# Values and gates of the short sequence: from ten column groups of 256 in the long mLSTM to six of 430 in the long attention

## The chip, the cores and the metric

The kernel runs on one core of a Trainium2 chip. The metric is the device time of one execution in microseconds (us); three runs of the kernel before are given. A separate profiled execution supplies the trace, with its own time.

The engines are named as the profile names them: PE is TensorE (matmuls), PEld its weight loads, DVE is VectorE, ACT is ScalarE, POOL is GpSimd, and SP is the engine whose queue issues most DMAs.

## The reference

One encoder layer is computed for two sequences, `x_prompt` (1024 tokens, called A or long here) and `x_sample` (512 tokens, B or short), all in float32 with a width of 1024:

```python
h = rms_norm(x, pre_w)
cols = h @ w_in                                  # 1024 columns in, 12,304 out
m_qk, m_v, m_o, m_z, m_i, m_f, a_qkv, a_z, gate = split(cols)
y_m = mlstm_mixer(m_qk, m_v, m_o, m_i, m_f, ...) * silu(m_z)      # conv of 3 over m_qk, two directions, chunks of 128
y_a = dilated_attention(a_qkv, rel_table) * silu(a_z)             # three dilations, 8 heads each, width 64
p_m, p_a = y_m @ w_pm, y_a @ w_pa
g = sigmoid(gate)
out = (g[0] * p_m + g[1] * p_a) @ w_out
return x + rms_norm(out, post_w)
```

The change touches three slices of `cols` for the short sequence: the gates `m_i, m_f` (16 columns), the mLSTM's values `m_v` (1024 columns) and the attention's values (1536 columns of `a_qkv`): 2576 columns in all.

## The kernel before

Every float32 product of the dense part is made of three matmuls on parts in the matmul's reduced float type: each operand is split in a high part (ACT copies, rounding) and a low part (DVE subtracts), and `mm3` (L193 to L198) issues high x high, high x low and low x high. In the profile these are the lines L196, L197 and L198.

The program runs in stages. First the dense products of A, with a two-level fast scheme for blocks of four (from the start to about 950 us). Then four stages in which a scan or an attention leads and the rest is filled in: the long mLSTM (`N.mlstm(A, ...)`, L1840), the long attention (`N.attend(A, ...)`, L1845), the short mLSTM (L1855) and the short attention (L1870), and an end of projections.

*The fill.* `Fill` (L114 to L174) is a list of units. A unit is one weight tile or several and a generator; each `yield` is a step. The leading stage calls `fill(share)` at fixed places of its round, and `fill.stage(steps, shares)` says how many steps a stage is to make in all. The numbers are `STEPS = (310, 232, 194, 290, 86)` (L1643), and `SHORT = 736` (L1642) counts all steps of the short sequence's own units. The long mLSTM has 64 rounds (4 heads, 8 chunks, two directions), each of which makes its fill in thirds; the long attention has 96 rounds of one tile each and three more to drain, with one share each (`att_round`, L1382). PE and SP run in the order in which the program is written; the other engines' order comes from the framework's planner.

*The weights of the fill.* `load_w` (L244) fetches a raw tile through `N.side` (SP's queue in the two mLSTM stages, POOL's in the long attention) into one of two `wraw` buffers. `split_w` (L251) splits it into one of the places `wsplit`: ACT writes the high part (L256), DVE the low part (L257). There are three places. `Fill.load` (L125) keeps the split tiles at most two ahead of those taken, and not more than there are places beyond `base`; the raw fetch is one more ahead.

*The short units* (`short_units`, L788 to L835), in order: 8 units of attention queries and keys (`att`), ten value units, 4 of `az`, 6 of `att`, 16 convolutions (`conv`), 8 pairs of `z` and `o` (together they make the gated factor G), 10 of `att`, and 16 output gates. All but the value units have eight steps with one weight tile of 128 columns, which is the stationary operand, and three matmuls of 512 columns a step. They write a PSUM bank of `ps_d`, of which there are two.

*The value units* (`value_unit`, L752 to L786): here the tokens are stationary and the weights move. Each of ten units has 256 columns (the first 272, with the gates) in two weight tiles of four rows of blocks each. For each of four token tiles it makes 8 x 3 matmuls, with a step after every second block: 16 steps of six matmuls a unit, 160 in all. After the last block `put` (L773) evacuates: for the mLSTM's values a high part (ACT, L779) and a low part (DVE, L780) go into one `sw` buffer and by DMA to `T.vs`; for the attention's a copy (ACT, L784) goes to `T.av`. `N.sw` rotates over four buffers; taking one issues a DMA still pending on it, and pending DMAs are issued by `tick` after `lag` rounds (two in the long mLSTM, three in the long attention).

*The convolution* (`conv_unit`, L676): POOL zeroes the two edge columns of `sraw` (L679, L680), ACT copies the PSUM bank into `sraw` (L797), then ACT L683, DVE L685 twice, ACT L686 and DVE L687. `sraw` is at the same time the only buffer of `N.sg`, which holds the factor of a `z` and `o` pair (L1835, L1836).

*Around it.* In the round of the long mLSTM, POOL, ACT and DVE prepare the next round (`front`, L1019) while PE makes the present one (`core`, L1054); the row values come by DMA (`rows`, L1009, tile `rw`), the state is updated on DVE (`cf`, L1085), ACT and DVE. In the long attention each tile goes through four stages, one round apart: products (`lg`), softmax (DVE L1287, ACT L1291), transposes (`pt`, L1298) and output (`o`, L1310). In both the last tile or head calls for the loads of the next stage.

## Time and profile before

| what | value |
|---|---|
| median of 3 runs | 2275.14 us (2273.26 to 2279.46) |
| profiled execution, its own time | 2274.2 us |
| its span, first to last instruction | 2272.4 us |
| PE busy | 2247.1 us, 99% of the span |
| DVE, ACT, POOL busy | 1502.9, 1130.3, 693.9 us |
| granted TensorE clock, mean | 0.998 |
| value units (first and last fetch of `w_v`) | 1005.1 to 1194.6 us |
| weights by DMA from `w_v` | 20 of 512 or 544 KB |

The profile's first part gives each engine's busy time, where matmuls are pipelined, so that a busy PE need not run at its best. The second cuts the span into forty slices. The fourth follows the work that ended last back to its start. The fifth groups instructions by line and shape. A window gives the busy time of each engine in a stretch of the span; the timeline gives single instructions with their start.

### The profile page before, as it was taken

What the parts mean: (1) busy time and instruction counts of PE and PEld (TensorE: products, weight loads), DVE (VectorE), ACT (ScalarE), POOL (GpSimd) and SP (SyncE); (2) the same over time, 40 slices, a digit from 0 to 9 for tenths busy, and PEclk for the clock granted to TensorE, in tenths of its full rate; (3) what the DMA queues carried; (4) which work ended last, traced back from release to release, by engine and by line L of the source; (5) the groups of instructions that cost most, each with busy time, mean ns of one, the idle gap of its engine ahead of it and who ended that gap; (6) DMA issues with size and microseconds to landing.
All of it is one profiled execution on the core that took longest, in us unless ns stands there. A gap on an engine that the chain in (4) does not pass through costs nothing.

```text
span 2272.4 us, 36227 instructions
## 1 busy us (share of the span) xinstructions
PE 2247.1 (99%) x12610; PEld 1970.5 (87%) x12610; DVE 1502.9 (66%) x2866; ACT 1130.3 (50%) x2376; POOL 693.9 (31%) x1002
## 2 busy tenths in 40 slices
PE   9999999999999999999999999999999999999998
PEld 8999888888888888889999889998888888888886
DVE  7765577678776556457776856665498844656673
ACT  6432244344444334366667666766665644545331
POOL 2000333333333223236566511011256522221220
PEclk9999999999999999999999999999999999999999
DMA  3652455543322223384674788987688698785661
GB/s 122 166 134 76 171 205 193 194 167 121 112 111 103 83 84 139 112 313 141 221 232 138 205 246 233 250 214 210 197 271 275 207 277 239 215 270 188 234 234 72
DMA packets 227952, 418.83 MB, mean 184 GB/s; under 512 B 24793, under 2 KB 131481, under 8 KB 227770
## 3 DMA queue, kind: packets, MB, share of 16 engines
q1 hardware_dynamic: 201144, 323.70, 45.3%
q0 software_dynamic: 23024, 80.23, 10.9%
q10 hardware_dynamic: 3602, 12.59, 1.4%
q8 instruction: 100, 1.64, 0.3%
q14 instruction: 82, 0.67, 0.1%
HBM read 296.44 MB, written 128.39 MB: 187 GB/s over the span
## 4 chain that ended last, share of the span: by engine, by line
PE 88%; issue 3%; DMA 3%; DVE 2%; ACT 2%; POOL 1%; SPq 0%; POOLq 0%; DVEq 0%; ACTq 0%
PE d L198 13%; PE d L197 13%; PE d L196 13%; PE dense L196 11%; PE dense L197 11%; PE dense L198 11%; PE o L1310 4%; PE pt L1298 2%; PE lg L1275 2%; DMA rw<-rw_a 1%; PE num L196 1%; PE num L198 1%; PE num L197 1%; PE a L996 1%; PE kv L196 1%
## 5 line engine op out<-in xcount | busy, mean ns | idle before, releaser
L196 PE MATMUL dense<-H,wh 128*128 128x512 f32 x672 | 277.0, 412 | 0.2 <-DVE r L1092 0.2
L198 PE MATMUL dense<-H,wl 128*128 128x512 f32 x672 | 263.7, 392 | 0.0
L197 PE MATMUL dense<-H,wh 128*128 128x512 f32 x672 | 263.1, 392 | 0.0
L197 PE MATMUL d<-Hl,phla 128*128 128x512 f32 x608 | 236.5, 389 | 0.0
L198 PE MATMUL d<-Hh,phla 128*128 128x512 f32 x608 | 236.5, 389 | 0.0
L196 PE MATMUL d<-Hh,phla 128*128 128x512 f32 x608 | 236.5, 389 | 0.0
L257 DVE TENSOR_TENSOR wl<-wraw,wh 128x1024 fp32r<-128x1024 f32 (+1 forms) x127 | 157.9, 1243 | 101.1 <-ACT wh L256 100.3
L256 ACT ACTIVATE wh<-wraw 128x1024 fp32r<-128x1024 f32 (+1 forms) x130 | 137.0, 1054 | 81.6 <-PE dense L197 31.2
L198 PE MATMUL d<-Hh,phlb 128*128 128x512 f32 x456 | 177.4, 389 | 0.0
L196 PE MATMUL d<-Hh,phlb 128*128 128x512 f32 x456 | 177.4, 389 | 0.0
L197 PE MATMUL d<-Hl,phlb 128*128 128x512 f32 x456 | 177.4, 389 | 0.0
L1287 DVE CUSTOM_DVE_ANT_0 ls<-lg,bias 128x256 f32<-128x256 f32 (+1 forms) x288 | 93.6, 362 | 122.7 <-PE lg L1275 58.1
L1291 ACT ACTIVATE ls<-ls,nm 128x256 f32<-128x256 f32 (+1 forms) x288 | 129.9, 453 | 84.0 <-DVE nm L1289 67.0
L635 POOL TENSOR_TENSOR psum_w<-pw_raw 128x512 f32<-128x512 f32 x38 | 56.1, 1477 | 363.8 <-DMA pw_raw<-w_in 202.2
L198 PEld LDWEIGHTS dense<-H,wl 128*128 128x128 f32 x672 | 126.2, 188 | 28.4
L197 PEld LDWEIGHTS dense<-H,wh 128*128 128x128 f32 x672 | 127.0, 189 | 16.4
L196 PEld LDWEIGHTS dense<-H,wh 128*128 128x128 f32 x672 | 126.6, 188 | 16.8 <-PE dense L198 0.6
L196 PE MATMUL d<-vhi,Hh 128*128 128x322 f32 x448 | 140.9, 314 | 0.3
L198 PE MATMUL d<-vhi,Hl 128*128 128x322 f32 x448 | 140.2, 313 | 0.5 <-DVE Hl L361 0.3
L197 PE MATMUL d<-vlo,Hh 128*128 128x322 f32 x448 | 139.7, 312 | 0.8 <-DVE vlo L434 0.8
L198 PEld LDWEIGHTS d<-Hh,phla 128*128 128x128 f32 x608 | 114.1, 188 | 23.7
L197 PEld LDWEIGHTS d<-Hl,phla 128*128 128x128 f32 x608 | 114.1, 188 | 23.7
(563 smaller groups left out, 6237.9 us busy)
## 6 DMA issues: line engine op xcount, KB each, us to landing
pw_raw<-w_in SPq DMA_DIRECT2D x76, 512.0 KB
aqk_a<-pwk SPq DMA_DIRECT2D x48, 512.0 KB
wraw<-w_in SPq DMA_DIRECT2D x45, 512.0 KB
wraw<-w_in POOLq DMA_DIRECT2D x31, 512.0 KB, 5.6
aqk_b<-sw SPq DMA_DIRECT2D x48, 256.0 KB
wraw<-w_pm POOLq DMA_DIRECT2D x24, 512.0 KB, 6.2
wraw<-w_out POOLq DMA_DIRECT2D x24, 512.0 KB, 4.0
wraw<-w_v SPq DMA_DIRECT2D x18, 512.0 KB
```

The costliest lines, as they stand in the source:

```text
L196: nc.tensor.matmul(out, lh, rh, start=start, stop=False)
L197: nc.tensor.matmul(out, lh, rl, start=False, stop=False)
L198: nc.tensor.matmul(out, ll, rh, start=False, stop=stop)
L256: self.splits = (nc.scalar.activation(hi[:, :n], raw[:, :n], AF.Copy), (self.lows or nc.vector).tensor_sub(lo[:, :n], raw[:, :n], hi[:, :n ...
L257: (self.lows or nc.vector).tensor_sub(lo[:, :n], raw[:, :n], hi[:, :n].bitcast(F32)))
L635: self.nc.gpsimd.tensor_add(s[:, 0], ws[1][:, 0], ws[1][:, 1])
L996: nc.tensor.matmul(p[:, c - c0], kT[:, ct, c * P:(c + 1) * P], qT[:, ct, c * P:(c + 1) * P], start=ct == 0, stop=ct == 1)
L1275: nc.tensor.matmul(lg[:, hh, c:c + w], q[hh][:, qs], z[:, k0:k0 + w], start=z is k[hh], stop=z is not k[hh])
L1287: nc.vector.tensor_tensor_reduce(out=ls[:, hh], in0=ts["lg"][hh], in1=bt[:, hh], scale=1.0, scalar=NEG, op0=OP.add, op1=OP.max, accum_out= ...
L1291: nc.scalar.activation(ls[:, hh], ls[:, hh], AF.Exp, bias=nm[:, hh:hh + 1], accum_out=ot[:, 128 + hh:129 + hh])
L1298: nc.tensor.transpose(pp[:, hh * nk + x], ts["ls"][:, hh, x * P:(x + 1) * P], self.ident)
L1310: nc.tensor.matmul(po[:, hh * 64:hh * 64 + 64], pt[:, hh * nk + x], v[:, kt[x], c0 + hh * 64:c0 + hh * 64 + 64], start=x == 0, stop=x == n ...
```

## The change

The ten value units become one unit, `value_units`, with six groups of 430 columns (the gates first, then the mLSTM's and the attention's values; 2580 columns of which the last four are padding and not computed). Each group has four weight tiles of two rows of blocks and 860 columns. The four token tiles of a group, and the groups after each other, overlap: a tile's second half is made in the same slots as the next tile's first half, so that two tiles are open in the two banks, and each weight tile is released after the fourth token tile has used it. A step is one block, three matmuls; there are 192.

For this unit two more places of split weights are laid over `X0` and `X1`, which the long mLSTM uses and the long attention does not, and they are dropped when the unit has ended (`extra`, `retired`).

The order of the short units changes: after the first 8 `att` units come eight convolutions (heads 0 and 1), each followed by one of the 6 `att` and first 2 `az` units; then two `az`, seven pairs of `z` and `o`, the values, the other eight convolutions, and the last pair. The rest is as it was. With `STEPS` the values begin 4 steps after the start of the long attention.

`sraw` is zeroed once, so the convolution no longer zeroes its edges, and `N.sg` gets a buffer of its own. The keys of the DMAs to `vs` and `av` no longer name the unit. The weight ring is 1024 columns wide, not 1088.

```diff
-VG = 256 + 16
-RING = 4 * VG
+VS, NV = 430, 2580
+RING = 1024
...
 # Fill.load
+            if any(self.net.wsplit[0][0] is x for x in self.net.retired):
+                self.net.wsplit.pop(0)
+                continue
...
-    def conv_unit(self, u, T, raw, w):
+    def conv_unit(self, u, T, raw, w, edges=True):
...
-        nc.gpsimd.memset(raw[:, 0:1], 0.0)
-        nc.gpsimd.memset(raw[:, S + 1:S + 2], 0.0)
+        for c in (0, S + 1) if edges else ():
+            nc.gpsimd.memset(raw[:, c:c + 1], 0.0)
...
+    def value_units(self, T):
+        nc = self.nc
+        groups = NV // VS
+
+        def put(t, lo, hi, ps):
+            ts = slice(t * P, (t + 1) * P)
+            if lo == 0:
+                nc.scalar.activation(self.gates_of(T, t), ps[:, 0:16].rearrange("p (j h) -> p j h", h=4), AF.Copy)
+            a0, a1 = max(lo, 16), min(hi, 16 + D)
+            if a0 < a1:
+                parts, x = [self.sw(F32R) for _ in range(2)], ps[:, a0 - lo:a1 - lo]
+                h, l = (z[:, :a1 - a0] for z in parts)
+                nc.scalar.activation(h, x, AF.Copy)
+                nc.vector.tensor_sub(l, x, h.bitcast(F32))
+                for i, z in enumerate((h, l)):
+                    self.put(("vs", T.S), T.vs[i, ts, a0 - 16:a1 - 16], z.bitcast(F32), parts[i])
+            a0 = max(lo, 16 + D)
+            if a0 < hi:
+                z = self.sw()
+                nc.scalar.activation(z[:, :hi - a0], ps[:, a0 - lo:hi - lo], AF.Copy)
+                self.put(("av", T.S), T.av[ts, a0 - 16 - D:hi - 16 - D], z[:, :hi - a0], z)
+
+        def make(weights):
+            fill = weights.__self__
+            w, p = {}, {}
+            for slot in range(8 * groups + 2):
+                for i in (slot // 2 - 1, slot // 2):
+                    g, t = divmod(i, 4)
+                    if not 0 <= i < 4 * groups:
+                        continue
+                    kp = slot - 2 * i
+                    if t == 0:
+                        w[g, kp] = [x.rearrange("p (k c) -> p k c", c=VS) for x in weights(g == kp == 0)]
+                    if kp == 0:
+                        p[i] = self.ps_d.tile([P, BLK], F32, name="dense")
+                    wk, ts = w[g, kp], slice(t * P, (t + 1) * P)
+                    lo, hi = VS * g, min(VS * (g + 1), 16 + D + 1536)
+                    for k in (2 * kp, 2 * kp + 1):
+                        h = self.hT[k // 4]
+                        self.mm3(p[i][:, :hi - lo], (h[0][:, k % 4, ts], h[1][:, k % 4, ts]),
+                                 (wk[0][:, k % 2, :hi - lo], wk[1][:, k % 2, :hi - lo]), k == 0, k == KT - 1)
+                        if k == KT - 1:
+                            put(t, lo, hi, p.pop(i))
+                        if t == 3 and k % 2:
+                            fill.release()
                         yield
...
+            self.retired = self.extra
+        return Unit([(self.a["w_v"][i], 2, VS) for i in range(4 * groups)], make)
...
 # short_units, conv
-                self.sg()
                 nc.scalar.activation(self.sraw[:, 1:1 + BLK], p, AF.Copy)
-                self.conv_unit(u, T, self.sraw, w)
+                self.conv_unit(u, T, self.sraw, w, False)
...
-        units = [x for u in range(4) for x in pair(u)] + [self.value_unit(u, T) for u in (0, 4, 1, 5, 2, 6, 3, 7, 8, 9)]
-        units += [az(i) for i in range(4)] + [x for u in range(4, 7) for x in pair(u)]
-        for h in range(4):
-            units += [conv(u + 2 * h + ct) for u in (U_MQ, U_MK) for ct in range(2)]
+        units = [x for u in range(4) for x in pair(u)]
+        others = [x for u in range(4, 7) for x in pair(u)] + [az(i) for i in range(4)]
+        zo = [x for i in range(8) for x in (z_unit(i), o_unit(i))]
+        convs = [conv(u + 2 * h + ct) for h in range(4) for u in (U_MQ, U_MK) for ct in range(2)]
         for i in range(8):
-            units += [z_unit(i), o_unit(i)]
+            units += convs[i:i + 1] + others[i:i + 1]
+        units += others[8:] + zo[:14] + [self.value_units(T)] + convs[8:] + zo[14:]
...
-SHORT = 736
-STEPS = (310, 232, 194, 290, 86)
+SHORT = 768
+STEPS = (316, 260, 192, 290, 86)
...
-                sraw = sp.tile([P, BLK + 2], F32R, name="sraw")
-                N.sg, N.sraw = Rot(N, [sraw[:, :BLK]]), sraw.bitcast(F32)
+                N.sraw = sp.tile([P, BLK + 2], F32, name="sraw")
+                nc.gpsimd.memset(N.sraw, 0.0)
+                N.sg = Rot(N, [sp.tile([P, BLK], F32R, name="sg")])
...
                 N.side = nc.gpsimd
+                extra = [N.take(x) for x in ("X0", "X1")]
+                extra = [[x[:, 1024 * i:1024 * (i + 1)] for i in range(2)] for x in extra]
+                N.extra = [x[0] for x in extra]
+                N.wsplit += extra
...
                 N.side = nc.sync
+                assert len(N.wsplit) == 3
```

More of the change, by code (lines that the diff above doesn't have):

```diff
@@ L750, in unit @@
         return Unit([(self.a["w_in"][u],)], make)
-    def value_unit(self, u, T):
+    def value_units(self, T):
         nc = self.nc
-        W = VG if u == 0 else 256
-        srcs = [((self.a["w_v0"][kh] if u == 0 else self.a["w_v"][2 * u + kh]), 4, W) for kh in range(2)]
-        def make(weights):
-            w = [[x.rearrange("p (k c) -> p k c", c=W) for x in weights(kh == 0)] for kh in range(2)]
-            for t in range(T.n):
-                ps = self.ps_d.tile([P, BLK], F32, name="dense")
-                ts = slice(t * P, (t + 1) * P)
-                for k in range(KT):
-                    wh, wl = w[k // 4]
-                    hi, lo = self.hT[k // 4]
-                    self.mm3(ps[:, :W], (hi[:, k % 4, ts], lo[:, k % 4, ts]), (wh[:, k % 4], wl[:, k % 4]), k == 0,
-                             k == KT - 1)
-                    if k == KT - 1:
-                        put(t, ts, ps)
-                    if k % 2:
-                        yield
-        def put(t, ts, ps):
-            if u == 0:
-                nc.scalar.activation(self.gates_of(T, t), ps[:, 256:VG].rearrange("p (j h) -> p j h", h=4), AF.Copy)
-            if u < 4:
-                of = self.sw(F32R)
-                z = of.rearrange("p (a c) -> p a c", a=2)
-                nc.scalar.activation(z[:, 0], ps[:, :256], AF.Copy)
-                nc.vector.tensor_sub(z[:, 1], ps[:, :256], z[:, 0].bitcast(F32))
-                self.put(("vs", T.S, u), T.vs[:, ts, 256 * u:256 * u + 256].rearrange("a t c -> t a c"), z.bitcast(F32), of)
-            else:
-                z = self.sw()
-                nc.scalar.activation(z[:, :256], ps[:, :256], AF.Copy)
-                self.put(("av", T.S, u - 4), T.av[ts, 256 * (u - 4):256 * (u - 3)], z[:, :256], z)
-        return Unit(srcs, make)
```

10 lines of the change are left out of this document (4 added, 6 removed).

## The prediction

> **What bounds the kernel now.** First I read the page: engines' busy time and the chain that ended last.
>
> ```profile
> span 2272.4 us, 36227 instructions
> ...
> PE 2247.1 (99%) x12610; PEld 1970.5 (87%) x12610; DVE 1502.9 (66%) x2866; ACT 1130.3 (50%) x2376; POOL 693.9 (31%) x1002
> ...
> PE 88%; issue 3%; DMA 3%; DVE 2%; ACT 2%; POOL 1%; SPq 0%; POOLq 0%; DVEq 0%; ACTq 0%
> ```
>
> TensorE is busy 2247.1 of 2272.4 us, and 88% of the chain is its own work. Only two things can change the time: how long TensorE needs for its work, and the gaps in it. The change lives in three stages, so I read the stages next, in windows, where the clock is full throughout (columns: length, then busy time of PE, PEld, DVE, ACT, POOL with instruction counts, clock, DMA share, GB/s).
>
> ```profile
> 1005.00:1060.00 55.00, 54.12 (x375) 50.08 (x374) 40.62 (x83) 37.71 (x95) 31.37 (x52) 1.00 0.58 194
> 1060.00:1245.00 185.00, 184.69 (x1530) 182.77 (x1530) 130.61 (x282) 124.28 (x317) 110.92 (x186) 1.00 0.58 192
> 1245.00:1310.00 65.00, 63.43 (x372) 55.34 (x371) 51.18 (x101) 40.66 (x99) 37.83 (x60) 1.00 0.76 213
> 1310.00:1330.00 20.00, 20.00 (x109) 17.07 (x108) 11.24 (x33) 10.53 (x28) 4.19 (x9) 1.00 0.83 240
> 1330.00:1600.00 270.00, 270.00 (x1783) 244.93 (x1782) 160.88 (x559) 184.06 (x550) 27.42 (x71) 1.00 0.85 229
> 1600.00:1630.00 30.00, 30.00 (x185) 26.55 (x183) 14.58 (x64) 19.26 (x69) 4.61 (x16) 1.00 0.54 167
> 1630.00:1800.00 170.00, 165.85 (x956) 143.65 (x954) 142.30 (x310) 104.31 (x246) 95.84 (x154) 1.00 0.78 255
> ```
>
> The first three rows are the long mLSTM, where the 256-column values run now. PE idles 0.88 + 0.31 + 1.57 = 2.76 us there. The next three are the long attention: no idle time at all, with ACT at 184/270 = 0.68 and the DMA engines at 0.85. So the attention holds no gap to win, and the mLSTM 2.76 us.
>
> **The matmuls that change shape.** The groups by shape give the counts; durations there overlap, so the cost of one is the distance between starts in the timeline (start, duration).
>
> ```profile
> L196 PE MATMUL dense<-wh,H 128*128 128x256 f32 x288 | 83.4, 290 | 0.0
> ...
> L196 PE MATMUL dense<-wh,H 128*128 128x272 f32 x32 | 9.5, 298 | 0.0
> ```
>
> ```profile
> 1120.84 0.28 PE L196 MATMUL dense<-wh,H 128*128 128x256 f32 x1
> ...
> 1124.42 0.60 PE L1005 MATMUL a<-ident,K 128*128 128x128 f32 x4
> ```
>
> ```profile
> 1404.29 0.40 PE L197 MATMUL dense<-H,wh 128*128 128x512 f32 x1
> ...
> 1406.15 1.00 PE L1310 MATMUL o<-K,pts 128*128 128x64 f32 x8
> ```
>
> ```profile
> 250.00:300.00 50.00, 50.00 (x222) 41.43 (x221) 31.34 (x39) 16.13 (x21) 15.38 (x12) 1.00 0.43 165
> ```
>
> There are three such lines (L196 to L198), hence 864 matmuls of 256 columns and 96 of 272. Between 1120.84 and 1124.42 lie 30 matmuls of 256 or 258 columns: 3.58/30 = 119.3 ns each. In the attention eight of 512 columns take 1.86 us, 232.5 ns each; in the undisturbed early stage 50/222 = 225.2 ns. After the change there are 480 matmuls of 430 columns and 96 of 426 (the last group stops at column 2576). The columns are the same, 247,296; only 384 starts fall away.
>
> Before: 864 x 119.3 = 103.1, and 96 at 126.4 (119.3 plus 16 columns of 0.442) = 12.1; together 115.2 us. After, by the straight line from 119.3 to 232.5: 196.2 and 194.5 ns, 112.8 us, a gain of 2.4. By the line to 225.2: 191.3 and 189.6 ns, 110.0 us, a gain of 5.2. I take the middle, **3.8 us**. The bounds: priced per column like the 256 ones (200.4 ns) nothing is won (0.1 lost); priced per column like 225.2/512 (189.1 ns) 6.4 is won.
>
> The Trainium skill speaks against this term: TensorE: Matmul & The Clock Gate, Back-to-back issue gap, gives N/2.4 + 2.5 ns, so a fixed cost of only 2.5 ns a matmul; by it the gain is an estimated 0.9 us. Its 109.2 ns for 256 columns disagrees with the 119.3 measured, so the measurement decides.
>
> **The fill order.** A step is one yield of a fill unit. The long mLSTM takes 310 steps now (64 att, 160 values of six matmuls, 32 az, 48 att, 6 conv); then 316 (64 att, 144 of conv, att and az mixed, 108 z and o), all of three 512-column matmuls. In PE time: 160 x 6 x 0.120 + 150 x 0.69 = 219 us against 316 x 0.69 = 218. The long attention goes from 232 steps to 260 (4 z/o, 192 values, 64 conv), the short mLSTM from 194 to 192 with the same kinds. So every dense matmul but the values' only changes place, and costs TensorE the same.
>
> **What moves onto the other engines.** Rows of DVE, first in the long mLSTM, then in the long attention, and of ACT in the attention (behind the bar: busy us, mean ns of one).
>
> ```profile
> L780 DVE TENSOR_TENSOR sw<-dense,sw 128x256 fp32r<-128x256 f32 x16 | 6.7, 420 | 2.4 <-ACT sw L779 2.4
> ...
> L697 DVE SCALAR_TENSOR_TENSOR sw<-sw,dense 128x512 f32<-128x512 f32 x4 | 2.7, 678 | 0.0
> ```
>
> ```profile
> L685 DVE SCALAR_TENSOR_TENSOR sw<-sraw,cws,sw 128x512 f32<-128x512 f32 x32 | 24.0, 749 | 2.0 <-ACT sw L683 1.1
> ...
> L687 DVE SCALAR_TENSOR_TENSOR sw<-sw,sw 128x512 f32<-128x512 f32 x16 | 11.0, 688 | 4.6 <-ACT sw L686 4.6
> ```
>
> ```profile
> L683 ACT ACTIVATE sw<-sraw,cws 128x512 f32<-128x512 f32 x16 | 13.0, 811 | 0.0
> L686 ACT ACTIVATE sw<-sw 128x512 f32<-128x512 f32 x16 | 10.0, 626 | 2.8 <-DVE sw L685 2.7
> L797 ACT ACTIVATE sraw<-dense 128x512 f32<-128x512 f32 x16 | 9.3, 582 | 0.0
> ```
>
> *Long mLSTM.* DVE loses 16 x 0.42 = 6.7 us and gains eight convs of 2 x 0.749 + 0.688 = 2.19 (17.5) and 13 z/o of 0.68 (8.8): about +20 on 222.4 busy us of 305, from 0.73 to 0.79. Weight splits stay (39 then 39). The row 1245:1310 stands at 51.18/65 = 0.79 already and loses 1.57 us, 2.4%; 1060:1245 at 0.71 loses 0.31. If the whole 250 us lost 2.4%, that would be 6.0 against 1.88 now: +4.1. If the load does no harm it is 0, and -1.9 if both rows' gaps went. The chain of that window says which is nearer:
>
> ```profile
> 1252.98 10.84 DMA rw<-rw_a
> ...
> 1268.56 0.68 DVE sw L697
> 1269.24 0.67 DVE cf L1085
> 1269.96 0.39 PE kv L196
> ```
>
> The late cf follows a row load of 10.84 us, beside the first loads for the attention, which stay where they are; DVE adds one 0.68 us operation. I take **+1.5**.
>
> *Long attention.* It loses about seven convs (each 2.02 us of ACT, 2.19 of DVE) and six z/o pairs; the values bring 24 short evacuations. So ACT and DVE get lighter, but PE had no gap there, so that is worth 0. The two memsets per conv that go away lie on POOL, busy 27 of 270 us: 0. The sg tile of its own frees conv from waiting for a z/o put: 0 for PE likewise. New writes (7.3 MB of values for some 3.5 of conv and G) add 3.8 MB to 270 us at 229 GB/s, 6%: DMA share some 0.90, still not full. SP issues some 18 more puts, three ticks late, with the loads of the next pair behind them; it waits then only for data three rounds old.
>
> Two waits are new. First, two tiles alternate in two PSUM banks, so a bank is needed again after 4 steps, not 8. By the windows the stage is 320 us for 99 rounds, 3.2 us each; at 260/96 = 2.7 steps a round, 4 steps are 4.8 us. ACT and DVE copy out in an estimated 1.1 us (0.5 and 0.6 for 430 columns, between the rows of 256 and 512), if neither waits. The group across the border of vs and av needs three sw buffers a tile of four, so it rewrites a buffer about 9.6 us after its last use, when its put, three ticks late, has just left. Second, weights come in bursts of four, one per 4.8 us, where now each unit of 8 steps asks for one, fetched a unit ahead.
>
> ```profile
> L248 POOL DMA_DIRECT2D wraw<-w_in x26: 537/537/747, 1319.4 to 1591.2; - x26
> ...
> DMA to landing us min/median/max: 3.7/6.0/10.2
> ```
>
> Twice per group (the fourth piece, and the next group's first) a split stands on ACT 4.8 us after its fetch: it blocks ACT for 1.2 us at the median landing and 5.4 at the longest, with the exponentials of the softmax queued behind it and the transposes on PE behind those. PE itself needs the piece two slots later, and the softmax is one round ahead, 3.2 us: a median load is hidden. Ends 0 and 26 (twelve loads, 2.2 us each beyond that round); nearest to the median, I take **+1.0** for both waits.
>
> *Sum:* -3.8 + 1.5 + 1.0 = -1.3 us. The profiled execution took 2274.2 us (1.8 around its span), 0.9 below the median of 2275.14. So **2272.9 us**.
>
> **Rivals.**
> *Weight loads were the bound of the values.* 182.77 of 185 us have a weight load under way in 1060:1245, against 41.43 of 50 beside 512 columns. Then the wider matmul runs at the cheapest column shown, 6.4 us are won, and with the mLSTM's heavy stretch relieved 1.5 of its gaps: 2274.2 - 7.9 = 2266.3. Against it: 512-column matmuls keep a rest over the pure per-column price too, and the gaps name DMA and DVE. The Trainium skill (Perfetto Trace Analysis, Identifying the Most-Contended Engine) would judge TensorE by this weight-load share; the trace, with 98.8% there, allows it.
> *DVE bounds the long mLSTM.* All of +4.1, plus 1.0: 2274.2 - 3.8 + 5.1 = 2275.5.
> *Nothing is won:* 430 columns cost as per column now: 2274.2 + 0.1 + 2.5 = 2276.8.
> *ACT blocked by bursts, slower.* Where landings exceed 4.8 + 3.2 = 8.0 us, each costs up to 2.2 us; with six of the twelve at 10.2, 13.2 us: 2274.2 - 3.8 + 1.5 + 13.2 = 2285.1. For it: ACT at 0.68, and landings up to 10.2 now. Against it: the median of 6.0.
>
> **How the numbers follow.** About 0.3%, 6.8 us, is what a measurement of this kernel can tell from no change. The forecast gets 0.50, weight loads 0.14, DVE 0.10, nothing won 0.04, bursts 0.22. Only the weight-load case lies beyond 0.3% below, with a little of the forecast's lower edge: faster 0.16. Bursts and a little of DVE: slower 0.24. The rest, 0.60, is the same. The range takes in the fast case and the bursts' price, 2265.5 to 2287.
>
> **What would show it.** Starts of 430-column matmuls 190 to 197 ns apart confirm the first term; under 189, the weight-load case; 200, none. PE idle in the long mLSTM near 4 us with DVE near 0.79 confirms the second. In the long attention, PE idle of about 1 us; many waits of ACT L256 for wraw, and of PE pt for ls, would be the bursts. If PE waits for dense banks, the evacuation term was wrong.

## The result, and the profile after

Five runs of the changed kernel give a median of 2285.82 us (2282.39 to 2290.49), five of the kernel before 2274.28 us (2273.26 to 2279.46): a ratio of **1.0047, 95% interval 1.0036 to 1.0057**. The kernel became slower by 11.5 us; forecast was 1.3 us faster than its profiled time. The profiled execution after took 2285.52 us with a span of 2283.6, so the two spans differ by 11.2 us.

The page of the kernel after, its span, busy times and chain:

```profile
span 2283.6 us, 35432 instructions
...
PE 2251.0 (99%) x12226; PEld 1965.3 (86%) x12226; DVE 1498.0 (66%) x2866; ACT 1129.0 (49%) x2368; POOL 691.7 (30%) x975
...
PE 86%; DMA 4%; issue 3%; DVE 3%; ACT 2%; POOL 2%; SPq 0%; POOLq 0%; DVEq 0%; ACTq 0%
```

DVE, ACT and POOL do no more than before in the whole program, and TensorE is busy only 3.9 us longer. So the loss is mostly waiting, and it has to be looked for by stage. For that I cut both spans at the first and last `num` and `lg` matmuls. The windows of the kernel before: fill ahead of the long mLSTM, long mLSTM, long attention, short mLSTM, end; the short attention, left out, takes 281.9 us in both (columns as in the prediction: length, then PE, PEld, DVE, ACT, POOL busy, clock, DMA share, GB/s):

```profile
950.00:995.10 45.10, 44.75 (x238) 37.99 (x237) 16.55 (x27) 21.68 (x39) 13.49 (x23) 1.00 0.70 245
995.10:1309.40 314.30, 311.54 (x2324) 296.32 (x2323) 228.34 (x477) 206.77 (x519) 181.68 (x300) 1.00 0.63 201
1309.40:1625.70 316.30, 316.30 (x2049) 285.29 (x2048) 184.17 (x648) 211.56 (x635) 33.58 (x88) 1.00 0.83 226
1625.70:1816.00 190.30, 186.16 (x1074) 161.47 (x1073) 158.31 (x349) 115.53 (x276) 104.79 (x172) 1.00 0.76 246
...
2097.90:2272.40 174.50, 162.18 (x725) 132.03 (x723) 103.38 (x177) 51.10 (x90) 37.08 (x67) 0.97 0.53 181
```

The same stages of the kernel after:

```profile
950.00:996.70 46.70, 45.48 (x241) 38.28 (x240) 16.78 (x27) 22.00 (x39) 13.60 (x22) 1.00 0.69 239
996.70:1317.00 320.30, 313.00 (x1859) 274.72 (x1858) 245.41 (x499) 215.44 (x516) 185.47 (x298) 0.99 0.59 189
1317.00:1639.30 322.30, 318.81 (x2130) 301.99 (x2129) 161.99 (x623) 198.61 (x624) 32.47 (x63) 0.99 0.86 229
1639.30:1826.30 187.00, 185.87 (x1076) 162.09 (x1075) 161.83 (x355) 119.21 (x283) 101.19 (x174) 1.00 0.78 252
...
2108.20:2283.60 175.40, 162.38 (x725) 131.93 (x723) 103.15 (x177) 51.10 (x90) 37.35 (x67) 0.98 0.53 180
```

Compare the length of each row (the second number): +1.6, **+6.0**, **+6.0**, -3.3, then 0 in the short attention, +0.9. Then length less PE: TensorE's idle time in the long mLSTM goes from 2.76 to 7.30 us, in the long attention from 0 to 3.49. Two stages lost about the same. In the first DVE has 17 us more to do, in the second 22 us less.

**The long mLSTM.** What TensorE waited for there, in the kernel after (what waited, for what, then us in all, times, longest):

```profile
PE num L200 <- DVE X L1117: 3.1, 2, 1.5
PE a L1129 <- ACT hn L1122: 2.1, 2, 1.9
PE kv L200 <- DVE cf L1104: 1.3, 2, 0.9
PE num L200 <- ACT X L1114: 0.7, 1, 0.7
```

and in the kernel before:

```profile
PE kv L196 <- DVE cf L1085: 1.9, 2, 1.0
PE num L196 <- DVE X L1098: 0.6, 1, 0.6
PE dense L197 <- DVE wl L257: 0.3, 1, 0.3
```

X, hn and cf belong to the scan itself: X reads the bank of `num` into the sum of both directions, hn is the normalised output. The timeline of DVE around two of the longest waits, in the kernel after (start, duration):

```profile
1153.18 0.15 DVE L1112 RECIPROCAL r<-r 128x1 f32<-128x1 f32 x1
1153.26 0.74 DVE L689 SCALAR_TENSOR_TENSOR sw<-sraw,cws,sw 128x512 f32<-128x512 f32 x1
1153.92 0.48 DVE L1117 SCALAR_TENSOR_TENSOR X<-num,r,X 128x256 f32<-128x256 f32 x1
```

X's other operand r is ready at 1153.33, and a tap of a moved convolution (L689) stands between: X starts at 1153.92, some 0.6 us later. That is a part of the wait of 1.54 us that follows, not all of it. The next matmuls on TensorE, same kernel:

```profile
1154.54 0.36 PE L200 MATMUL num<-V1a,sch 128*128 128x258 f32 x1 [1.54 <-DVE X L1117]
...
1159.09 0.44 PE L1129 MATMUL a<-ident,hn 128*128 128x128 f32 x2 [1.86 <-ACT hn L1122]
...
1160.78 0.63 PE L200 MATMUL dense<-H,wh 128*128 128x512 f32 x1
...
1163.34 0.31 PE L200 MATMUL kv<-V0a,kh 128*128 128x258 f32 x1
```

The first two rows are the waits. The second, 1.86 us for hn, does not come from DVE directly. The rows of POOL and ACT before it:

```profile
1157.89 0.60 POOL L1121 TENSOR_TENSOR r<-r,mhalf 128x1 f32<-128x1 f32 x1
...
1158.53 0.51 ACT L1122 ACTIVATE hn<-X,r 128x256 f32<-128x256 f32 x1 [0.52 <-POOL r L1121]
```

The sum of squares that this r is made from is ready at 1154.94 (ACT L1119), one step after the late X; then r stands in POOL's queue behind the preparation of the next rounds. So the delay passes from one engine's queue to the next.

The last two rows of TensorE show what the waits bring with them: six 512-column matmuls start 0.427 us apart ((1163.34 - 1160.78)/6), against 0.23 before the gap. The clock that was granted, as the window of this stretch shows it (third number from the end), is half:

```profile
1160.00:1163.40 3.40, 3.40 (x11) 2.71 (x11) 2.89 (x8) 3.00 (x9) 1.45 (x3) 0.50 0.67 175
```

These six matmuls and three slow `num` ahead of them cost some 1.5 us. The half clock returns from 1480.8 to 1484.2, in the attention.

**The long attention.** Its shape that is new, TensorE of the kernel after:

```profile
1400.26 0.35 PE L201 MATMUL dense<-wl,H 128*128 128x430 f32 x1
...
1401.82 1.00 PE L1329 MATMUL o<-K,pts 128*128 128x64 f32 x8
```

Eight matmuls of 430 columns lie between: 1.56/8 = 195 ns each. Now ACT in the same stage:

```profile
1470.63 0.32 ACT L770 ACTIVATE sw<-dense 128x180 fp32r<-128x180 f32 x1
1476.39 0.92 ACT L260 ACTIVATE wh<-wraw 128x860 fp32r<-128x860 f32 x1 [5.45 <-DMA wraw<-w_v]
...
1477.38 0.37 ACT L777 ACTIVATE sw<-dense 128x250 f32<-128x250 f32 x1
```

ACT stands 5.45 us at the split of a weight that has not landed, and the copy that frees the dense bank (L777, the second half of the evacuation that L770 began) comes behind it. TensorE waits for exactly that, and for the softmax's transposed tiles (pts). Its waits in this stage, which had none before:

```profile
PE dense L200 <- ACT sw L777: 1.3, 1, 1.3
PE o L1329 <- DVE pts L1322: 1.1, 1, 1.1
PE o L1329 <- ACT pts L1320: 0.8, 2, 0.6
PE lg L1294 <- DVE ot L1306: 0.3, 1, 0.3
```

ACT's waits for raw weights there, same kernel, of which the kernel before has none:

```profile
ACT X L260 <- DMA wraw<-w_v: 13.0, 4, 5.1
...
ACT wh L260 <- DMA wraw<-w_v: 10.9, 3, 5.4
```

Seven waits, 23.9 us: the bursts that the prediction priced as a rival. The weights took longer to land than the fetches that the prediction went by (3.7/6.0/10.2 us); for `wraw`, 1320 to 1560, kernel after:

```profile
DMA to landing us min/median/max: 3.2/7.0/11.0
```

Nearly all of TensorE's waits here, 3.3 of 3.5 us, lie close behind three of ACT's stands: 0.3 and 0.6 us at 1349 and 1356, behind stands of 5.1 and 1.2 us that end at 1346.4 and 1355.1; and 1.3 and 1.1 us at 1477 and 1479, around the one of 5.45 us that is shown.

### The profile page after: what moved, and what is told of

Read it like the earlier page. It is cut to its first block, busy times and chain, and to the rows that moved or that the text cites. A ratio compares the mean times of both kernels' runs of the same rounds, so it can differ in the third digit from the quotient of the medians.

```text
span 2283.6 us, 35432 instructions
## 1 busy us (share of the span) xinstructions
PE 2251.0 (99%) x12226; PEld 1965.3 (86%) x12226; DVE 1498.0 (66%) x2866; ACT 1129.0 (49%) x2368; POOL 691.7 (30%) x975
## 3 DMA queue, kind: packets, MB, share of 16 engines
q1 hardware_dynamic: 199096, 323.55, 45.1%
## 4 chain that ended last, share of the span: by engine, by line
PE 86%; DMA 4%; issue 3%; DVE 3%; ACT 2%; POOL 2%; SPq 0%; POOLq 0%; DVEq 0%; ACTq 0%
PE d L202 13%; PE d L201 13%; PE d L200 13%; PE dense L200 10%; PE dense L202 10%; PE dense L201 10%; PE o L1329 4%; PE pt L1317 2%; PE lg L1294 2%; PE num L202 1%; PE num L200 1%; PE num L201 1%; PE a L1015 1%; PE kv L200 1%; PE kv L201 1%
## 5 line engine op out<-in xcount | busy, mean ns | idle before, releaser
L200 PE MATMUL dense<-H,wh 128*128 128x512 f32 x664 | 270.9, 408 | 0.0
L201 PE MATMUL dense<-H,wh 128*128 128x512 f32 x664 | 260.7, 393 | 0.0
L261 DVE TENSOR_TENSOR wl<-wraw,wh 128x1024 fp32r<-128x1024 f32 (+1 forms) x121 | 147.3, 1217 | 99.0 <-ACT wh L260 98.3
L260 ACT ACTIVATE wh<-wraw 128x1024 fp32r<-128x1024 f32 (+1 forms) x124 | 128.4, 1036 | 87.8 <-PE dense L201 25.7
L202 PEld LDWEIGHTS d<-Hh,phla 128*128 128x128 f32 x608 | 114.1, 188 | 23.7
L200 PEld LDWEIGHTS d<-Hh,phla 128*128 128x128 f32 x608 | 114.1, 188 | 23.7
```

Of the source, the lines that this page charges most:

```text
L200: nc.tensor.matmul(out, lh, rh, start=start, stop=False)
L201: nc.tensor.matmul(out, lh, rl, start=False, stop=False)
L202: nc.tensor.matmul(out, ll, rh, start=False, stop=stop)
L260: self.splits = (nc.scalar.activation(hi[:, :n], raw[:, :n], AF.Copy), (self.lows or nc.vector).tensor_sub(lo[:, :n], raw[:, :n], hi[:, :n ...
L261: (self.lows or nc.vector).tensor_sub(lo[:, :n], raw[:, :n], hi[:, :n].bitcast(F32)))
```

## The experiments

Two theories. **The scan theory:** the convolutions and z/o factors moved into the long mLSTM put work on DVE, whose short operations for the scan then come late; so the loss comes with the move, whatever the columns of a group. **The burst theory:** the weights of the values come four at a time, ACT blocks on them in the long attention, and that is the loss. Times below are medians; ratios are to runs of the kernel before on the same chip, made beside them, with a 95% interval. Stage lengths and idle times are cut like those above and come from the one profiled execution of each kernel.

### move_only: the order of the units without the groups of 430

The ten units of 256 columns and three places of weights stay, at the place and in the order of the change:

```diff
-STEPS = (310, 232, 194, 290, 86)
+STEPS = (316, 228, 192, 290, 86)
...
+        for i in range(8):
+            units += convs[i:i + 1] + others[i:i + 1]
+        units += others[8:] + zo[:14] + [self.value_unit(u, T) for u in (0, 4, 1, 5, 2, 6, 3, 7, 8, 9)] + convs[8:] + zo[14:]
```

> The kernel before, with its ten value units of 256 columns and three places, but in the new order: eight convolutions mixed into the long mLSTM, values in the long attention (STEPS 316, 228, 192). Scan theory (the convolutions' ACT and DVE work stands between the operations of the scan, and PE waits for the scan): the long mLSTM is some 6 us longer than before, the whole about 2281 us. Burst theory (ACT stands on splits whose weights come four at a time): nothing of it here, so within 2 us of before, about 2275.

2290.09 us, 1.0067 [1.0055, 1.0079]: the move alone costs all of it and more. The long mLSTM takes 320.1 us with 7.5 idle, as after. So the loss of the long mLSTM needs no groups of 430. The long attention takes 320.1 us, but with only 0.4 idle: TensorE is busy there 319.7 us, 3.4 more than in the kernel before, since the values in columns of 256 take an estimated 2.5 us more (960 matmuls at 120 and 125 ns) than the 164 steps of other units that left (some 0.69 us each). ACT stands at no value weight in this stage, and TensorE's waits of the kernel after (3.5 us idle) are gone with that. The change is 4 us faster than this version by the medians; the short mLSTM alone, whose units are the same, is 6.1 us shorter (187.0 against 193.1).

### three_raws: a third raw buffer in the long attention

The change, with one raw weight buffer more (in the spare tile `apart`) and fetches two ahead until the values end:

```diff
-            self.fetch(len(self.ready) + 1)
+            self.fetch(len(self.ready) + self.deep)
...
+                self.wraw.insert(0, apart)
+                fill.deep, self.third = 2, apart
```

> The changed kernel with a third buffer for raw weights during the values (laid in a spare tile of the long attention) and the fetch two tiles ahead of the split, not one. Burst theory: the 24 us that ACT and the split wait for raw weights in the long attention fall under 6, and about 6 us of time go: 2279 to 2280. Scan theory: the long attention's loss is not from there, no change from 2285.8 beyond 1.5 us.

2284.24 us, 1.0038 [1.0025, 1.0051]. ACT's waits for raw weights in the long attention, with this edit:

```profile
ACT X L263 <- DMA apart<-w_v: 6.2, 1, 6.2
```

with two more of 1.9 and 0.8 us: 8.9 us instead of 23.9, not the under 6 that was expected. The attention got 1.6 us shorter (320.7 us, 2.5 idle), and the interval overlaps that of the change. This does not clear the bursts, for what is left still comes from one. ACT stands at `apart` until 1349.40, and TensorE's only wait in the stage follows:

```profile
1351.67 1.18 PE L1321 MATMUL pt<-ident,ls 128*128 128x128 f32 x4 [2.50 <-ACT ls L1314]
```

From 1350.3 to 1357.1 the granted clock is 0.50. So the third buffer takes away the stand at 1471 to 1476 with its two waits, and lengthens the one before it in the stage from 5.1 to 6.2 us, which then costs nearly as much.

### weights_sp: the weights through the other queue

The change, without `N.side = nc.gpsimd`, so that in the long attention SP's queue, not POOL's, fetches weights:

```diff
-                N.side = nc.gpsimd
```

> The changed kernel with the weights of the long attention fetched through SP's queue, not POOL's. If the fetch stands in POOL's queue behind waiting bias copies and that makes the burst late, 2280 to 2283 us. If the burst is late because a transfer takes longer than one slot, no gain: 2284 to 2288, the more since SP's queue has waits of its own.

2288.36 us, 1.0062 [1.0051, 1.0074]: the attention takes 325.9 us with 6.6 idle, 4.4 of them in one wait behind a stand of ACT of 6.3 us at `wraw<-w_in`. The other queue is no help.

### bare_convs: the moved convolutions without their arithmetic

The change, where the eight convolutions in the long mLSTM leave out filter and activation and store a copy:

```diff
+                if 2 * (u % 8 // 2) < 4:
+                    y = w()
+                    nc.scalar.activation(y, self.sraw[:, 1:1 + BLK], AF.Copy)
+                    self.put(("qk", T.S, u), T.qk[u], y, y)
+                    return
```

> The changed kernel; of the eight convolutions in the long mLSTM only the copy out of PSUM and the store are made, their three-tap filter and activation (one ACT and two DVE filter operations, ACT tanh, DVE product) are left out. Scan theory: PE's idle time in the long mLSTM falls from 7.3 to about 3 us and the whole to about 2280. Burst theory: 2284 to 2286.

2279.02 us (11 runs, 2273.75 to 2280.73), 1.0013 [1.0004, 1.0021]. The row of one window, first of the kernel after, for comparison with the next ones:

```profile
1000.00:1310.00 310.00, 302.70 (x1796) 265.56 (x1795) 238.76 (x482) 209.87 (x502) 181.47 (x291) 0.99 0.60 191
```

and of bare_convs:

```profile
1000.00:1310.00 310.00, 309.19 (x1853) 273.61 (x1852) 224.94 (x473) 212.98 (x511) 181.67 (x301) 1.00 0.61 194
```

Idle time falls from 7.3 to 0.8 us and the long mLSTM from 320.3 to 310.4 us, 3.9 less than before the change. Without the convolutions' arithmetic the loss of this stage is gone. By the medians it is worth some 7 us of the 11.5 (ratio 1.0047 to 1.0013); the profiled run is the fastest of its eleven. The long attention takes 321.0 us here.

### conv_no_dve and conv_no_act: which engine's part

In the same eight convolutions, once DVE's three operations are left out, and once ACT's first tap and tanh:

```diff
+        light = not edges and 2 * (u % 8 // 2) < 4
...
-        for i in (1, 2):
+        for i in () if light else (1, 2):
...
+        if not light:
+            nc.vector.scalar_tensor_tensor(y, th, 1.0, y, op0=OP.add, op1=OP.mult)
```

```diff
+        if not light:
+            nc.scalar.activation(y, raw[:, 0:S], AF.Identity, scale=cw[:, 0:1], bias=cw[:, 3:4])
...
+        if not light:
+            nc.scalar.activation(th, y, AF.Tanh, scale=1.0 if u < U_MK else 16.0)
...
```

> The changed kernel; of the eight convolutions in the long mLSTM the three DVE operations (two filter taps, the product with the activation) are left out, the ACT ones stay. If DVE's share is the cause: PE's idle time in the long mLSTM falls from 7.3 to under 3 us, 2278 to 2280. If ACT's share is: 7 us stay, 2284 to 2286.

> The changed kernel; of the eight convolutions in the long mLSTM the first tap and the tanh on ACT are left out, the three DVE operations stay. If DVE's share is the cause: PE's idle time in the long mLSTM stays at 6 or more, 2283 to 2286. If ACT's share or the change between the two engines is: under 3 us, 2278 to 2280.

Without DVE's part 2280.34 us, 1.0019 [1.001, 1.0028]; without ACT's 2290.06, 1.0058 [1.0045, 1.0071]. The window of conv_no_dve:

```profile
1000.00:1310.00 310.00, 309.40 (x1857) 273.99 (x1856) 224.03 (x473) 217.40 (x516) 179.44 (x298) 1.00 0.61 194
```

and of conv_no_act:

```profile
1000.00:1310.00 310.00, 302.11 (x1790) 265.71 (x1789) 239.30 (x480) 201.19 (x486) 180.83 (x289) 0.99 0.60 190
```

DVE at 224 us: 0.6 idle, the gain of bare_convs in full. DVE at 239 and ACT relieved by 9: 7.9 idle, no gain. It is DVE's part. One other way from DVE's operations to TensorE is not the cause by itself: SP's queue, which also fetches the scan's data, stands at the stores of the convolutions. It does so in both kernels, first after, then conv_no_dve, where the store follows ACT:

```profile
SPq L216 <- DVE sw L691: 49.1, 5, 13.9
```

```profile
SPq L216 <- ACT sw L691: 40.6, 6, 10.8
```

40.6 us of such stands go with 0.6 us of idle time. In its profiled run conv_no_dve took 327.4 us in the long attention, against 321.0 in bare_convs, though that stage's work is the same in both; I come back to it.

### dve_load and dve_free: the kernel before, with more work for DVE

To see whether any work on DVE does this, the kernel before gets more of it in the long mLSTM, with nothing moved. Some 20 us were meant; by the stages' rows the first form adds 11.9 us (240.2 against 228.3), the second 24.3. First by repeating the subtraction of each evacuation of the mLSTM's values, and a product by 1.0 for the attention's:

```diff
-                nc.vector.tensor_sub(z[:, 1], ps[:, :256], z[:, 0].bitcast(F32))
+                for _ in range(3):
+                    nc.vector.tensor_sub(z[:, 1], ps[:, :256], z[:, 0].bitcast(F32))
...
+                nc.vector.tensor_scalar(z[:, :256], z[:, :256], 1.0, None, op0=OP.mult)
```

> The kernel before with DVE work added where the values are evacuated in the long mLSTM: the low part of 16 tiles is written three times instead of once, and each of 24 attention tiles is multiplied by 1.0 in place; some 20 us in short operations of 256 columns, as much as the change brings there. Load theory (the long mLSTM suffers because DVE is fuller): PE's idle time there rises from 2.8 to 6 or 7 us, the whole to 2278 or 2279. Blocking theory (what hurts is how the convolution's long operations on ACT and DVE stand between those of the scan): at most 1.5 us, 2275 to 2276.

2282.54 us, 1.0024 [1.0013, 1.0035], 6.7 us idle in the long mLSTM. But the longest of its waits is another one:

```profile
PE dense L196 <- DVE sw L781: 4.4, 3, 2.1
```

The repeated subtractions read the dense bank, so they keep it from TensorE: 4.4 us of the loss are that, and the run doesn't separate the theories. The second form works on the tile that is already written and touches no bank:

```diff
+                nc.vector.scalar_tensor_tensor(of, of.bitcast(F32), 1.0, of.bitcast(F32), op0=OP.mult, op1=OP.max)
...
+                nc.vector.scalar_tensor_tensor(z[:, :256], z[:, :256], 1.0, z[:, :256], op0=OP.mult, op1=OP.max)
```

> The kernel before with some 22 us of DVE work added in the long mLSTM that touches no PSUM bank: each evacuated value tile is combined with itself once in its SBUF buffer (16 of 512, 24 of 256 columns). Load theory: PE's waits for the scan's results there (num, kv, a: 2.5 us in before) rise to 5 or more, the whole to 2278 to 2280. Blocking theory (the convolution's dependent chain over ACT and DVE is what hurts): at most 1.5 us more, 2275 to 2276.

2284.36 us, 1.0039 [1.0025, 1.0053]. Its long mLSTM:

```profile
995.60:1318.70 323.10, 315.19 (x2323) 297.76 (x2322) 252.66 (x517) 206.41 (x519) 184.29 (x300) 0.99 0.62 195
```

The stage takes 323.1 us, 8.8 more than before, 7.9 idle. The stages behind it are those of the kernel before to 0.2 us (316.3, 190.5, 281.9, 174.5). So 24 us of work on DVE that TensorE doesn't wait for cost 8.8 us here, more work and more loss than the change brings (17 and 6.0). The stores do wait for it: SP's queue stands 37.8 us at the added L781, and this run alone doesn't separate that from DVE's queue. TensorE waits mostly for the scan's cf on DVE, as it should if DVE's queue is what is late:

```profile
PE kv L196 <- DVE cf L1084: 2.7, 2, 2.3
PE kv L196 <- DVE cf L1087: 1.6, 3, 0.9
```

### conv_halves: is it the length of one operation?

The change, with each of the moved convolutions' operations cut into two halves of 256 columns, so that a short operation of the scan stands behind less:

```diff
+        cuts = [(0, S)] if edges else [(0, S // 2), (S // 2, S)]
...
+            for a, b in cuts:
+                nc.vector.scalar_tensor_tensor(y[:, a:b], raw[:, i + a:i + b], cw[:, i:i + 1], y[:, a:b], op0=OP.mult, op1=OP.add)
```

> The changed kernel; each of the five filter and activation operations of a convolution is made in two halves of 256 columns, the same work in pieces half as long. Blocking theory: shorter pieces let the scan's operations pass sooner, PE's idle time in the long mLSTM falls from 7.3 to under 5 us, 2282 to 2284. Load theory: more fixed cost on ACT and DVE, 2286 to 2290.

2289.98 us, 1.0058 [1.0037, 1.008]; the long mLSTM idles 9.4 us, with DVE at 242.06 of 310 where the change has 238.76. Shorter pieces don't help, and they add some load.

### steps_only: the kernel before with other shares

The kernel before with the numbers of steps that move_only has, no unit moved:

```diff
-STEPS = (310, 232, 194, 290, 86)
+STEPS = (316, 228, 192, 290, 86)
```

> The kernel before with only the numbers of steps changed (316, 228, 192 in place of 310, 232, 194): the same units in the same order, shared out among the stages a little differently. If the loss of the change is that any new sharing out spoils an order of the other engines that happened to fit, the time moves by 4 us or more (2279 and up). If the loss needs the convolutions in the long mLSTM, within 2 us of before: 2274 to 2277.

2279.93 us, 1.0016 [1.0007, 1.0024]: above the 2274 to 2277 that was expected if the loss needs the convolutions, and within the 2279 and up of the other case. So a new sharing out alone costs 3.6 us by the ratio (1.6 to 5.5), with no unit moved. It does not cost them where the change loses most: the long mLSTM idles 1.9 us, less than before. In the profiled run, one of the faster ones (2277.13), the fill ahead is 1.1 us longer, the long mLSTM, with six steps more, 1.7, the end 1.8, and the short mLSTM 1.9 shorter. bare_convs (1.0013) and conv_no_dve (1.0019) come down to about this ratio; whether what is left in them is the same re-sharing was not tried.

### split and split_raws: only the attention's values moved

The mLSTM's values stay in the long mLSTM in units of 256 columns; the attention's values go to the long attention in three groups of 512, with all convolutions behind them. `N.sg` shares `sraw` again, as in the kernel before. The second has the third raw buffer of three_raws too.

```diff
-VS, NV = 430, 2580
+VG = 256 + 16
+VS, NV = 512, 1536
...
+        units += [self.value_unit(u, T) for u in range(4)] + others + zo[:14] + [self.value_units(T)] + convs + zo[14:]
```

> A version meant to keep the wide groups and lose the convolutions' place: gates and mLSTM values in four units of 256 columns in the long mLSTM as before, the attention's values in three groups of 512 columns in the long attention on five places of weights, all sixteen convolutions in the long attention, z and o in the long mLSTM. 288 matmul starts fewer than before. If the convolutions in the long mLSTM are the loss, that stage idles about 3 us again and the whole is 2272 to 2274; if any evacuation work there hurts as much, 2278 or more; bursts would cost about 2 us in the long attention.

> The same with the third buffer for raw weights and the fetch two tiles ahead. If bursts still cost in the long attention, 1 to 2 us less than without: 2271 to 2273; if not, the same.

2282.13 us, 1.0026 [1.0013, 1.004], and 2281.84 us, 1.0024 [1.0013, 1.0035]. The attention is as short as before in split (316.3 us, 1.0 idle; with groups of 512 columns ACT still stands up to 4.8 us at a weight). But the long mLSTM idles 5.3 and 5.6 us with DVE at only 225.09 of 310 in split, against 0.8 idle at 224.94 in bare_convs. So DVE's load isn't the only thing that counts there. The longest wait of split is 2.5 us for hn, as in the kernel after through r on POOL, and the chain before it runs through the load of a row of `rw`:

```profile
1155.12 4.42 DMA rw<-rw_a
```

POOL stands 1.3 us for this row, with r behind in its queue. The next, 2.1 us for cf, lies behind a stand of DVE of 2.9 us for a store of ym to finish. Here a queue stands for a DMA and is not full; why those DMAs are late in split, these runs don't show.

### before_relief, after_relief, relief_raws: a remedy that fails

If DVE is too full, POOL could take some of it: every third weight's low part in the long mLSTM. In the kernel before, in the change, and in the change with the third raw buffer:

```diff
+        self.count += 1
+        low = nc.gpsimd if self.relief and self.count % 3 == 0 else self.lows or nc.vector
...
-                       (self.lows or nc.vector).tensor_sub(lo[:, :n], raw[:, :n], hi[:, :n].bitcast(F32)))
+                       low.tensor_sub(lo[:, :n], raw[:, :n], hi[:, :n].bitcast(F32)))
```

> The kernel before; in the long mLSTM the low part of every third weight tile is subtracted on POOL (2.4 us each) instead of DVE (1.25 us), some 13 tiles, 16 us off DVE. Load theory: PE's idle time in the long mLSTM falls from 2.8 to about 1 us, 2272 to 2275. Blocking theory: DVE had room, and POOL's long operations now stand before the scan's own: 2276 to 2280.

> The changed kernel with the same relief of DVE. Load theory: DVE in the window 1000 to 1310 falls from 239 to about 223 us, PE's idle time in the long mLSTM from 7.3 to 3 or less, 2280 to 2282. Blocking theory, or POOL as full as DVE: no gain, 2285 or more.

> The changed kernel with both: the relief of DVE in the long mLSTM and the third raw buffer in the long attention. If the two losses are separate they add: 2278 to 2280. If not, as the better of the two alone.

2279.37 us, 1.0017 [1.0009, 1.0026]; 2293.28 us, 1.0072 [1.0059, 1.0086]; 2286.66 us, 1.0048 [1.0036, 1.006]. The first two are slower than without; the third is not told apart from three_raws (1.0038 [1.0025, 1.0051]). The groups of after_relief, first POOL, then DVE (busy us, mean ns of one, idle before):

```profile
L264 POOL TENSOR_TENSOR wl<-wraw,wh 128x1024 fp32r<-128x1024 f32 x11 | 26.5, 2409 | 10.7 <-ACT wh L263 10.7
```

```profile
L1073 DVE SCALAR_TENSOR_TENSOR kl<-K,col,kh 128x256 fp32r<-128x256 f32 x54 | 34.3, 636 | 5.8 <-ACT kh L1072 4.7
```

In the change without relief the same operation (L1070, x54) is busy 29.1 us, 539 ns each. Eleven subtractions leave DVE, 14 us at 1270 ns, and its busy time falls by 2 only (238.76 to 236.73 of 310), since its other operations get longer: kl alone takes 5.2 us more. POOL goes from 181.47 to 203.62 us, and it carries steps of the scan itself. The long mLSTM idles 10.6 us. In before_relief DVE does lose work (226.60 to 215.84 of 310), and the stage still idles 4.7 us instead of 2.8, 2.0 of them in one wait for hn, whose r POOL makes. No kernel of this study beats the one before.

## Why the prediction was wrong

The range, 2265.5 to 2287, holds the time; the sign was wrong. Point by point:

**The matmuls (-3.8).** Direction right, somewhat large. Starts 195 ns apart lie inside the 190 to 197 named as confirmation. Over all value matmuls the median distances between starts (120 and 125 ns before, 196 and 194 after) give 115.7 us before and 112.7 after, -3.0, since 430 columns stand on the line to 232.5, not between the two. About 1.5 us of it goes back: a 512-column matmul costs some 232 ns in the long mLSTM and 229 in the attention, and some 495 of them changed place in that direction. That the move of the dense steps costs TensorE nothing was thus wrong by this small sum. The weight-load rival is out: it needed 189 ns or less. The formula of the Trainium skill that was set against this term (TensorE: Matmul & The Clock Gate, Back-to-back issue gap) is given there for a single matmul by itself, not for a stream of them; by it the gain is 384 x 2.5 ns = 0.96 us, not 0.9.

**The long mLSTM (+1.5): the step that failed.** The load was seen rightly, +20 on DVE against +17 measured. What failed is "The late cf follows a row load of 10.84 us ... I take +1.5". I let one wait of one window stand for the cause of the whole stage, and took the value near its lower half. What the runs show in its place: the work on DVE delays the scan. In dve_free 24 us more on DVE alone cost 8.8 us, and in conv_no_dve, where DVE's part of the convolutions is left out, the stage idles 0.6 us. The measured cost is +6.0. Even the upper end, +4.1, was too low, and it is that of the rival "DVE bounds the long mLSTM", which got a chance of 0.10. Idle time rose by 4.5, near that rival's price; the rest is the half clock after the gaps (about 1.5), which no term held. The waits run through several queues (DVE, then POOL and ACT), and how much each adds is open; split idles 5.3 us at a low load of DVE.

**The long attention (+1.0): mis-sized, the second step that failed.** Measured +6.0: idle 3.5, half clock from 1480.8 to 1484.2 about 1.6, and some 0.9 us more of TensorE's busy time that I can tie to no row. The signs named for the bursts and for a wrong evacuation term came: waits of ACT for raw weights, and one of TensorE for a dense bank, here through the burst; the named wait of pt for ls came in other kernels (2.5 us in three_raws, 4.4 in weights_sp), in the change it was o for pts. The step that failed is "a median load is hidden ... nearest to the median, I take +1.0". The median landing was 7.0 us and not 6.0, and the median is not what costs: ACT's stands were as long as the prediction's own 1.2 to 5.4 us, and the largest of TensorE's waits stand around the one of 5.45 us. That the idle time is the bursts' is read from traces: it stands behind ACT's stands in after, bare_convs, conv_no_dve and three_raws, and move_only, where ACT has none at the values' weights, idles 0.4 us. No run takes all of these stands away and keeps the groups. What I called worth 0, that ACT and DVE get lighter there, was right.

The stage took 321.0 us in bare_convs and 327.4 in conv_no_dve with the same work. Idle time is 3.7 and 6.5 us of that, and conv_no_dve has two stretches of 3.4 us at half clock where bare_convs has none. Why the loads land better in one than in the other is open, and so is what the four sw buffers add.

**The rivals.** "Slower by bursts" gave 2285.1 and was met to 0.7 us, and that is luck: it had +1.5 for the long mLSTM and 13.2 for the bursts, where 6.0 and 6.0 were measured, and more than half of the loss, by the ratios (1.0047 against 1.0019 in conv_no_dve), comes from DVE's part of the convolutions in the long mLSTM. move_only, which has no groups, is slower still. "Nothing won" fails on the 195 ns.

**Not foreseen:** the short mLSTM gets 3.3 us shorter (4.1 idle before, 1.1 after), the fill ahead of the long mLSTM 1.6 us longer. The latter lies between 46.0 and 48.6 us in every kernel with the new order, against 45.1; but it is 46.2 with the new shares alone and 46.4 and 46.5 in before_relief and dve_load, which keep order and shares, so the order is not shown to be the cause. And re-sharing the steps costs by itself (steps_only). A small miss that moves no sum: SP issues 48 puts of the short sequence in the long attention against 27, 21 more and not 18.

## What to carry to other kernels

Price work that moves into a stage by how full the queues are in which that stage's own short operations stand, and not by what single gap the trace of before happens to name: 24 us more on an engine busy 73% of a scan cost 8.8 us here. It can be tried without the change: add the same load to the kernel before, on data that TensorE doesn't wait for and on no bank that another engine needs, and compare the busy times of whole stages to see how much was really added. And a stage without any idle time is no proof that it has room: where an engine works in order, a weight that lands late holds up the copy that frees a bank. Price a burst of loads by its late landings, not by the median one.

## What the hardware showed unexpectedly

*Half clock after short gaps.* In the kernel after, gaps of 1.54 and 1.86 us, 2.7 us of matmuls between them, were followed by 3.4 us at a granted clock of 0.50 (starts 0.427 against 0.23 us); gaps of 1.26 and 1.08 us at 1476 to 1480 by another 3.4 us. One gap can be enough: in move_only one of 1.86 us that ends at 1195.0, in conv_halves one of 2.18 us that ends at 1196.9 were each followed by 3.4 us at 0.50, with no other gap over 0.1 us in the 10 us before. The gap of 1.53 us before 1301.6 in the kernel after was not. The Trainium skill, TensorE: Matmul & The Clock Gate, What's actually happening, has the half rate follow on an idle window of about 3.4 us; here no gap before a stretch named above is that long, and the measurement decides. In the Trainium skill, the same page's section A second HAM failure mode: psum-queue depth-cycling has frequent small gaps make the clock swing; the pairs of gaps here are like that, the single ones of move_only and conv_halves are not.

*DVE's operations stretch.* A tap of the convolution takes 749 ns in the long attention of the kernel before and 747 in that of the kernel after. In the long mLSTM of the kernel after:

```profile
L689 DVE SCALAR_TENSOR_TENSOR sw<-sraw,cws,sw 128x512 f32<-128x512 f32 x16 | 14.7, 920 | 0.6 <-ACT sw L687 0.4
```

920 ns, 23% more, where POOL is busy 0.58 of the time instead of 0.11 and 0.10. With kl's 539 to 636 ns under relief, this goes with POOL's work beside it; the mechanism was not tried by itself.
